# Attention scores computed by each head on its own half of the array's rows, with keys stored without zeros

## The chip, the cores and the metric

The kernel runs on one core of a Trainium2 chip. A core has a matrix engine (TensorE, in the profile PE, with its weight loads as PEld), a vector engine (DVE), a scalar engine (ACT), a general engine (POOL) and SyncE (SP), which here issues the transfers. Every engine works through its own instructions in order; semaphores tie them together. TensorE multiplies a stationary operand (up to 128 x 128, loaded first) by a moving operand (up to 512 columns) and leaves the sum in PSUM, a memory of eight banks per partition. A bank holds 512 float32 values in each of the 128 partitions. DVE and ACT read PSUM and write SBUF, from which TensorE reads.

The metric is device time in microseconds (us). The kernel before has a median of 1146.4 us in three runs (1146.05 to 1146.9).

## The reference

A trunk of four layers over x of 256 tokens by 1024 features, all float32. Each layer is a token mixer, then a squared-ReLU MLP of width 4096, both with an RMSNorm ahead and a residual sum behind. The mixers are, in order: differential attention (layers 0 and 3), MoBA attention (layer 1; with 256 tokens there is one block, so it is plain causal attention over 16 heads) and sliding-window attention with sinks (layer 2: 16 query heads, 2 key heads). All heads have 64 features. What the change touches is the product of queries and keys:

```python
HEAD_DIM = 64
# differential attention: 8 heads, each with two score maps
s = jnp.einsum('bqhcd,bkhcd->bhcqk', qi, k).astype(f32)
s = jnp.where(causal, s, -jnp.inf)
p = jax.nn.softmax(s, axis=-1)
p = p[:, :, 0] - lam * p[:, :, 1]
return jnp.einsum('bhqk,bkhe->bqhe', p.astype(v.dtype), v)
...
# MoBA: the own block
s_own = jnp.einsum('bhqd,bhkd->bhqk', qi, k_own).astype(f32)
...
# sliding window with sinks
s = jnp.einsum('bnqkgd,bnjkd->bnkgqj', qb, k2).astype(f32)
s = jnp.where(mask[None, :, None, None], s, -jnp.inf)
m = jnp.maximum(jnp.max(s, axis=-1, keepdims=True), sink)
e = jnp.exp(s - m)
p = (e / (jnp.sum(e, axis=-1, keepdims=True) + jnp.exp(sink - m))).astype(v.dtype)
```

So every layer has 16 score maps of 256 queries by 256 keys over 64 features.

## The kernel before

**Precision.** Every large product is made of three: an operand is split into a high part in the type float32r and the remainder, also float32r, and high x high, high x low and low x high are summed in PSUM. `stage` splits a weight piece of 1 MB in two halves of 128 x 1024 (ACT writes `whi`, line 80; DVE writes `wlo`, line 81). `put_q` and `put_k` do the same for queries and keys.

**A mixer layer.** `mixer_layer` runs projections with `proj` (line 296; 48 matmuls, two row blocks t of 24). Layers 0, 1 and 3 have six projections, four of which make the queries and keys of four heads c (`qk`, 512 columns), and two the values. Layer 2 has one for keys and values and four (256 columns) for queries. Behind each, DVE applies the rotary embedding (`rope`, lines 304 to 309). `turn` transposes the result on TensorE (`p_qk`, line 465), so that features lie on the partitions: partitions 0 to 63 hold one score map's features, 64 to 127 the other's. "Pair" is used here for the two maps that share a 128-partition tile; a pair is one `SC` step.

**Scores of a pair.** `new_keys` allocates two tiles `kpad` (high and low) and POOL fills with zeros the half of the partitions that is not a map's own (line 369). `put_k` copies each map's 64 partitions into its own block of columns. So a full 128-row matmul of a pair's queries with `kpad` gives both maps side by side: the zeros cancel the other map's features. Queries 0 to 127 see 128 keys, thus 256 columns; queries 128 to 255 see 256 keys, thus 512 columns. With three products each (`mm3`, lines 271 to 273) a pair costs six matmuls, into two banks `p_s0` and `p_s1`, one for each block of queries. For both maps and both query blocks, DVE adds the mask and reduces (`ns`, line 336), ACT takes the exponential with its sum (line 339). `diff_head` combines the two maps of a pair (lines 384 to 389), `head_block` divides by the sums (lines 424 to 427); `transposed` turns the result on TensorE (`p_t`, line 354), and the product with the values follows (`p_av`, lines 360 to 362 and 436). Line 436 writes one map's 64 output features to each half of the PSUM partitions: its matmuls use half of the array's columns each.

**Order.** The program text gives steps of attention out among the matmuls of the next projection: `proj` takes a list `midway`, run after its 24th matmul, and `plan` names for each projection what runs midway and what behind it: `QK` (transposes and splits), `SC` (scores and softmax), `TR` (transposes), `AV` (values), `OUT`. Layer 2 does it with `step`, `first` and `second`. A scheduler of the framework then settles each engine's order from this; the order of the built program differs from the text in places. The projections and the MLP share four banks `acc`; `p_qk`, `p_s`, `p_t`, `p_av`, `p_o` and `p_up` share four banks `wk`.

Of the kernel before, what the change touches and what calls it, by code (L numbers as in the profile page):

```python
# [12 lines left out]
F32R = mybir.dt.float32r  # L13
I32 = mybir.dt.int32
AF = mybir.ActivationFunctionType
OP = mybir.AluOpType
AX = mybir.AxisListType

P = 128
D = 1024  # L20
S = 256
NT = S // P
DEPTH = 4
FF = 4096
HD = 64
# [9 lines left out]
def f(ap):  # L35
    return ap.bitcast(F32)
# [3 lines left out]
def trunk(ctx: ExitStack, tc: tile.TileContext, xT, gains, lams, swa_row, fng, weights, out):  # L40
# [8 lines left out]
    def bank(tag, name):  # L49
        return ps.tile([P, 512], F32, tag=tag, name=name, bufs=4)  # L50

    def room(j, shape, name, dt=F32):

        return sb.tile(shape, dt, tag=f"slot{j}", name=name, bufs=1)
# [214 lines left out]
    def mm3(out, lh, ll, rh, rl, start, stop, **kw):  # L269

        T.matmul(out, lh, rh, start=start, stop=False, **kw)  # L271
        T.matmul(out, lh, rl, start=False, stop=False, **kw)  # L272
        T.matmul(out, ll, rh, start=False, stop=stop, **kw)  # L273
# [39 lines left out]
    def scores(q, k, mask, sinks):  # L313


        p0, p1 = bank("wk", "p_s0"), bank("wk", "p_s1")
        (qh, ql), (kh, kl) = q, k
        for p, t, n in ((p0, 0, P), (p1, 1, S)):
            o = p[:, :2 * n].rearrange("p (h m) -> p h m", h=2)
            a = slice(P * t, P * t + P)  # L320
            mm3(o, qh[:, a], ql[:, a], kh[:, :, :n], kl[:, :, :n], True, True)
        out = []
        if sinks is not None:
            es = tiny.tile([P, 2 * NT], F32, tag="es", name="es", bufs=2)
        scored[0] += 1
        pair_e = room(4 + scored[0] % 2, [P, 2, 3 * P], "e")
        ls = tiny.tile([P, 2 * NT], F32, tag="l", name="l", bufs=5)
        for c in range(2):
            ns = sb.tile([P, 3 * P], F32, tag="ns", name="ns", bufs=2)
            nm = tiny.tile([P, NT], F32, tag="nm", name="nm", bufs=4)  # L330
            l = ls[:, NT * c:NT * c + NT]
            e = pair_e[:, c]
            mk = mask[:, :, :].rearrange("p a b -> p (a b)")
            for t, p, n in ((0, p0, P), (1, p1, S)):
                s = slice(0, P) if t == 0 else slice(P, 3 * P)
                V.tensor_tensor_reduce(ns[:, s], p[:, n * c:n * c + n], mk[:, s], op0=OP.add, op1=OP.min,  # L336
                                       scale=-1.0, scalar=3.0e38 if sinks is None else sinks[c][1],
                                       accum_out=nm[:, t:t + 1])
                A.activation(e[:, s], ns[:, s], AF.Exp, bias=nm[:, t:t + 1], scale=-1.0,  # L339
                             accum_out=l[:, t:t + 1])  # L340
            if sinks is not None:
                A.activation(es[:, NT * c:NT * c + NT], nm, AF.Exp, bias=sinks[c][0])
            out.append((e, l))
        if sinks is not None:
            V.tensor_tensor(ls, ls, es, op=OP.add)
        return out, pair_e, ls
# [11 lines left out]
    def times_v(o, et, v):  # L358
# [1 line left out]
        T.matmul(o(0), et[:, 0:P], v(0), start=True, stop=True)  # L360
        T.matmul(o(1), et[:, P:2 * P], v(0), start=True, stop=False)
        T.matmul(o(1), et[:, 2 * P:3 * P], v(1), start=False, stop=True)

    def new_keys():

        kpad = [room(10 + x, [P, 2, 2, S], f"kpad{'hl'[x]}", F32R) for x in range(2)]
        for x in range(2):
            for h in range(2):
                G.memset(f(kpad[x][HD * (1 - h):HD * (1 - h) + HD, :, h, :]), 0.0)
        return kpad  # L370

    def part(b, n=1):

# [66 lines left out]
        V.tensor_tensor(both[:, 1], p[:, :S], f(both[:, 0]), op=OP.subtract)  # L440
        parts.append(both)

    line = []

    def step(block=None):


        line.append(block)
        if block is not None:
            next(block)  # L450
        if len(line) > 1 and line[-2] is not None:
            next(line[-2])
        if len(line) % 2 == 0:
            for x in line[:-2]:
                if x is not None:
                    next(x, None)
            line[:-2] = [None] * len(line[:-2])

    def turn(src, n):

        p = bank("wk", "p_qk")
        for b in range(n):
            for t in range(NT):
                at = S * b + P * t
                T.transpose(p[:, at:at + P], src(b, t), ident)  # L465
        return p[:, :S * n].rearrange("p (b m) -> p b m", m=S)
# [8 lines left out]
        V.scalar_tensor_tensor(q[1], p, 0.125, f(q[0]), op0=OP.mult, op1=OP.subtract)  # L475
        return q

    def put_k(k, p, n):
        for h in range(2):
            s = slice(HD * h, HD * h + HD)  # L480
            A.activation(k[0][s, :n, h, :], p[s], AF.Copy)
            V.tensor_tensor(k[1][s, :n, h, :], p[s], f(k[0][s, :n, h, :]), op=OP.subtract)

    def mixer_layer(i, n):
        mixer, slot = i % 3, i // 3
        r = norm_factor(n)
        parts = []
        kpad = new_keys()
        if mixer == 2:
            bias = room(8, [P, 1024], "bias")  # L490
            rest = room(9, [P, 1024], "rest")
# [7 lines left out]
                V.scalar_tensor_tensor(kv[:, t, :], p[t], r[:, t:t + 1], rest[:, :256],  # L499
                                       op0=OP.mult, op1=OP.add)  # L500
            rope(kv[:, :, 0:P].rearrange("p t (s e) -> p t s e", e=HD), 2)
            put_k(kpad, turn(lambda b, t: kv[:, t, 0:P], 1), 1)
            kT = [x[:, 0] for x in kpad]
            first, second = [], []
            for c in range(4):
                p = proj(n, (256, 1), False, first)
                qn = room(c % 2, [P, NT, 256], "qn")
                for t in range(NT):
                    for h in range(2):
                        s = slice(P * h, P * h + P)  # L510
                        o = qn[:, t, :].rearrange("p (b h e) -> p b h e", h=2, e=HD)[:, :, h, :]
                        bs = bias[:, 512 * h + P * c:512 * h + P * c + P]
                        V.scalar_tensor_tensor(o, p[t][:, s].rearrange("p (b e) -> p b e", e=HD), r[:, t:t + 1],
                                               bs.rearrange("p (b e) -> p b e", e=HD), op0=OP.mult, op1=OP.add)
                rope(qn[:, :, :].rearrange("p t (s e) -> p t s e", e=HD), 4)
                for do in second:
                    do()
                qs = []

                def block(b, c=c, qs=qs, qn=qn):  # L520
                    if b == 0:
                        qs += put_q(turn(lambda b, t: qn[:, t, P * b:P * b + P], 2))
                    h = 2 * c + b
                    step(head_block(
                        parts, [x[:, b] for x in qs], kT, lambda m: kv[:, m, P:2 * P], band,
                        [(sink[:, h + 8 * s:h + 8 * s + 1], nsink[:, h + 8 * s:h + 8 * s + 1]) for s in range(2)],
                        h,
                    ))

                first, second = [lambda f=block: f(0)], [lambda f=block: f(1)]  # L530
        else:
            v = [room(8 + j, [P, NT, 512], f"v{j}") for j in range(2)]
            vdone = 0
            qk, qs, heads, pairs, ets, els = {}, {}, {}, {}, {}, {}

            def QK(c):

                qs[c] = put_q(turn(lambda j, t: qk[c][:, t, P * j:P * j + P], 2))
                put_k(kpad, turn(lambda j, t: qk[c][:, t, P * (2 + j):P * (2 + j) + P], 2), 2)

            def vh(h):
                return lambda m: v[h // 4][:, m, P * (h % 4):P * (h % 4) + P]

            def SC(h):
                q, k = [x[:, h % 2] for x in qs[h // 2]], [x[:, h % 2] for x in kpad]
                if mixer == 0:
                    if h % 2 == 0:
                        els[h // 2] = tiny.tile([P, 2 * NT], F32, tag="el", name="el")
                    heads[h] = diff_head(slot, q, k, els[h // 2][:, NT * (h % 2):NT * (h % 2) + NT])
                else:  # L550
                    heads[h] = head_block(parts, q, k, vh(h), causal, None, h)
                next(heads[h])
# [15 lines left out]
            def LAM(_):  # L568
                if i == 0:
                    lambdas()  # L570

            order = (0, 1, "v", 2, 3, "v") if mixer else (0, 1, "v", 2, "v", 3)
            plan = [[], [], [(QK, 0), (LAM, 0), (SC, 0)], [(SC, 1)], [(TR, 0), (QK, 1), (SC, 2)], [(TR, 1), (SC, 3)],
                    [(TR, 2)], [(TR, 3), (AV, 0), (AV, 1)], [(QK, 2), (SC, 4)], [(AV, 2), (AV, 3), (SC, 5)],
                    [(TR, 4), (QK, 3), (SC, 6)], [(TR, 5), (SC, 7)],
                    [(AV, 4), (AV, 5), (TR, 6), (TR, 7), (AV, 6), (AV, 7)]]
            if mixer == 0:
                plan[6:8] = [[(TR, 2), (AV, 0)], [(TR, 3), (AV, 1)]]
                plan[8:] = [[(AV, 2), (QK, 2), (OUT, 0), (SC, 4)], [(AV, 3), (SC, 5)], [(TR, 4), (AV, 4)],
                            [(OUT, 1), (TR, 5), (AV, 5)],  # L580
                            [(QK, 3), (SC, 6), (SC, 7), (OUT, 2), (TR, 6), (AV, 6), (TR, 7), (AV, 7)]]
            for at, c in enumerate(order):
# [16 lines left out]
            return parts, (lambda: OUT(3))  # L599
        for do in first + second:  # L600
            do()
        for _ in range(3):
            step()
        line.clear()
        return parts, lambda: None


# [295 lines left out]
```

## Time and profile before

| | |
|---|---|
| median of three runs | 1146.4 us |
| the profiled execution, whole | 1146.28 us |
| its span, first to last instruction | 1144.3 us |
| TensorE clock granted | 0.998 |
| moved by DMA | 198.66 MB |

A row of instructions reads: source line, engine, operation, tile written <- tiles read, partitions x elements, count, then busy time and mean duration. In a timeline the first two numbers are start and duration in us. Durations on TensorE overlap: a matmul starts before the one ahead of it has drained, so the cost of one is the distance to the start of the next. On DVE and ACT too a row starts a little before the row ahead has ended.

### The profile page before, as it was taken

Reading aid. Unit: us, or ns where it says so; the run is one execution under the profiler, and the core shown is the slowest. Engines: PE = TensorE matmul, PEld = TensorE weight load, DVE = VectorE, ACT = ScalarE, POOL = GpSimd, SP = SyncE. Lnnn points to the kernel's source line nnn. Section 1 sums busy time; section 2 is a strip of 40 time slices with the busy share of each in tenths; the row PEclk is TensorE's granted clock in tenths of the full one; section 3 lists DMA queues with packets and bytes.
Section 4 is the critical chain, followed back from the end, with each engine's and each line's share of the span. In section 5 each row is a group of like instructions: output and inputs, shape, how many; then the busy total and the mean of one; then the engine's idle time right before and its main releaser. Section 6 shows DMA issues by size and latency. Waiting matters only on the chain.

```text
span 1144.3 us, 17044 instructions
## 1 busy us (share of the span) xinstructions
PE 1133.7 (99%) x6560; PEld 987.0 (86%) x6560; DVE 827.9 (72%) x1608; ACT 660.6 (58%) x1207; POOL 11.4 (1%) x39
## 2 busy tenths in 40 slices
PE   9999999999999999999999999999999999999997
PEld 7789888888888888888899898888888889888886
DVE  7978977656676698766569887775667788777454
ACT  6866655544476665654446765554447676665342
POOL 1000000000000000000000000000000000000000
PEclk9999999999999999999999999999999999999999
DMA  9543455555544355555553346555553435555551
GB/s 327 198 147 117 165 201 190 194 201 185 185 141 148 117 184 187 195 200 191 184 208 111 111 148 221 184 185 189 188 202 127 151 139 164 192 195 169 186 182 37
DMA packets 30608, 198.66 MB, mean 174 GB/s; under 512 B 3520, under 2 KB 5184, under 8 KB 7360
## 3 DMA queue, kind: packets, MB, share of 16 engines
q1 hardware_dynamic: 30240, 197.06, 50.0%
q8 instruction: 51, 0.84, 0.3%
q10 hardware_dynamic: 288, 0.52, 0.1%
q14 instruction: 29, 0.24, 0.1%
HBM read 196.52 MB, written 1.05 MB: 173 GB/s over the span
## 4 chain that ended last, share of the span: by engine, by line
PE 95%; DVE 2%; DMA 1%; ACT 1%; issue 0%; SPq 0%; DVEq 0%
PE p_up L610 21%; PE p_in L296 18%; PE p_down L610 15%; PE p_up L611 11%; PE p_down L611 8%; PE p_last L273 3%; PE p_last L271 3%; PE p_last L272 3%; PE p_d L273 2%; PE p_d L272 2%; PE p_d L271 2%; PE p_t L354 1%; PE p_s L271 1%; PE p_qk L465 1%; DVE wlo L81 1%; PE p_av L436 1%
## 5 line engine op out<-in xcount | busy, mean ns | idle before, releaser
L81 DVE TENSOR_TENSOR wlo<-raw,whi 128x1024 fp32r<-128x1024 f32 (+1 forms) x374 | 447.0, 1209 | 206.0 <-ACT whi L80 204.9
L80 ACT ACTIVATE whi<-raw 128x1024 fp32r<-128x1024 f32 (+1 forms) x374 | 384.5, 1046 | 213.3 <-issue 111.1
L610 PE MATMUL p_up<-hg,whi 128*128 128x512 f32 x1024 | 356.9, 393 | 0.4
L611 PE MATMUL p_up<-hg,wlo 128*128 128x256 f32 x1024 | 284.9, 279 | 0.0
L610 PE MATMUL p_down<-uu,whi 128*128 128x512 f32 x768 | 266.4, 392 | 0.0
L610 PEld LDWEIGHTS p_up<-hg,whi 128*128 128x128 f32 x1024 | 191.5, 187 | 43.3 <-DVE hg L229 1.0
L611 PE MATMUL p_down<-uu,wlo 128*128 128x256 f32 x768 | 214.3, 279 | 0.0
L296 PE MATMUL p_in<-whi,hg 128*128 128x512 f32 (+1 forms) x736 | 211.3, 371 | 0.0
L611 PEld LDWEIGHTS p_up<-hg,wlo 128*128 128x128 f32 x1024 | 193.2, 189 | 0.5
L610 PEld LDWEIGHTS p_down<-uu,whi 128*128 128x128 f32 x768 | 143.7, 187 | 32.1
L296 PEld LDWEIGHTS p_in<-whi,hg 128*128 128x128 f32 x736 | 132.3, 188 | 22.8 <-DVE hg L229 0.6
L611 PEld LDWEIGHTS p_down<-uu,wlo 128*128 128x128 f32 x768 | 144.8, 189 | 0.0
L296 PE MATMUL p_in<-wlo,hg 128*128 128x512 f32 (+1 forms) x368 | 130.4, 369 | 0.5 <-DVE wlo L81 0.5
L685 ACT ACTIVATE uu<-u 128x512 fp32r<-128x512 f32 x64 | 40.5, 633 | 71.1 <-DVE u L683 71.1
L296 PEld LDWEIGHTS p_in<-wlo,hg 128*128 128x128 f32 x368 | 68.8, 189 | 12.7 <-DVE wlo L81 1.7
L616 ACT ACTIVATE cross<-p_up 128x256 f32<-128x256 f32 x128 | 47.9, 374 | 39.3 <-PE p_up L611 33.8
L228 ACT ACTIVATE hg<-hT,gn 128x256 fp32r<-128x256 f32 x64 | 31.6, 503 | 65.5 <-DVE hT L629 65.2
L339 ACT ACTIVATE e<-ns,nm 128x128 f32<-128x128 f32 (+1 forms) x128 | 56.9, 446 | 12.0 <-DVE nm L336 11.7
L686 DVE TENSOR_TENSOR uu<-u,uu 128x512 fp32r<-128x512 f32 x64 | 44.2, 691 | 21.5 <-ACT uu L685 21.5
L271 PE MATMUL p_d<-oo,whi 128*128 128x256 f32 x192 | 55.1, 287 | 0.0
L272 PE MATMUL p_d<-oo,whi 128*128 128x256 f32 x192 | 55.1, 287 | 0.0
L617 DVE TENSOR_TENSOR relu<-p_up,cross 128x256 f32<-128x256 f32 x128 | 53.5, 418 | 1.6 <-ACT cross L616 1.5
(182 smaller groups left out, 1246.3 us busy)
## 6 DMA issues: line engine op xcount, KB each, us to landing
raw<-in_weights SPq DMA_DIRECT2D x181, 1024.0 KB, 4.9
raw<-in_weights SPq DMA_DIRECT2D x8, 256.0 KB, 4.5
raw<-in_weights SPq DMA_DIRECT2D x4, 512.0 KB, 7.7
hT<-in_xT SPq DMA_DIRECT2D x8, 128.0 KB, 4.4
bias<-in_swa_row SPq DMA_DIRECT2D x1, 512.0 KB, 4.3
grow<-in_fng SPq DMA_DIRECT2D x1, 512.0 KB, 3.5
out<-res SPq DMA_DIRECT2D x4, 128.0 KB, 2.1
out<-res ACTq DMA_DIRECT2D x2, 256.0 KB, 2.2
```

Of the source, the lines that this page charges most:

```text
L80: A.activation(hi[:, s], raw[:, s], AF.Copy)
L81: V.tensor_tensor(lo[:, s], raw[:, s], f(hi[:, s]), op=OP.subtract)
L271: T.matmul(out, lh, rh, start=start, stop=False, **kw)
L272: T.matmul(out, lh, rl, start=False, stop=False, **kw)
L273: T.matmul(out, ll, rh, start=False, stop=stop, **kw)
L296: T.matmul(out[t], n.both[k // 2][:, k % 2, x, P * t:P * t + P], r3(kb)(parts[k // kb][w])[:, k % kb, :], start=fresh, stop=k == 7 and x + ...
L339: A.activation(e[:, s], ns[:, s], AF.Exp, bias=nm[:, t:t + 1], scale=-1.0, accum_out=l[:, t:t + 1])
L610: T.matmul(r3(2)(p), hi, x, start=start, stop=False, skip_group_check=True)
L611: T.matmul(p[:, :S], lo, x[:, 0], start=False, stop=stop, skip_group_check=True)
L616: A.activation(cross, p[:, S:], AF.Copy)
L617: V.tensor_tensor(out, p[:, :S], cross, op=OP.add)
L686: V.tensor_tensor(both[:, :, 1], r3(2)(u), f(both[:, :, 0]), op=OP.subtract)
```

## The change

Each map's scores are computed with its own 64 partitions of queries and keys alone, on half of the array's rows; the two maps of a pair write different banks, `ps_h[0]` and `ps_h[1]`, and stand alternately in the text. Keys are stored as they come from the transposes, without zeros, in one tile `khl`, and two buffers of it alternate. In the order, the two pairs of a head group are given out together (`SC` of both midway); layer 2 loses `step` and gives transposes and scores of two pairs out in `blocks_of`, the values in `values_of`.

```diff
     def scores(q, k, mask, sinks):
-        p0, p1 = bank("wk", "p_s0"), bank("wk", "p_s1")
+        ps_h = [bank("wk", f"p_s{c}") for c in range(2)]
         (qh, ql), (kh, kl) = q, k
-        for p, t, n in ((p0, 0, P), (p1, 1, S)):
-            o = p[:, :2 * n].rearrange("p (h m) -> p h m", h=2)
+        for cols, t, n in ((slice(0, P), 0, P), (slice(P, 3 * P), 1, S)):
             a = slice(P * t, P * t + P)
-            mm3(o, qh[:, a], ql[:, a], kh[:, :, :n], kl[:, :, :n], True, True)
+            for x, y, first, last in ((qh, kh, True, False), (qh, kl, False, False), (ql, kh, False, True)):
+                for c in range(2):
+                    r = slice(HD * c, HD * c + HD)
+                    T.matmul(ps_h[c][:, cols], x[r, a], y[r, :n], start=first, stop=last, skip_group_check=True)
...
-            for t, p, n in ((0, p0, P), (1, p1, S)):
+            for t in range(NT):
                 s = slice(0, P) if t == 0 else slice(P, 3 * P)
-                V.tensor_tensor_reduce(ns[:, s], p[:, n * c:n * c + n], mk[:, s], op0=OP.add, op1=OP.min,
+                V.tensor_tensor_reduce(ns[:, s], ps_h[c][:, s], mk[:, s], op0=OP.add, op1=OP.min,
...
-    def new_keys():
-
-        kpad = [room(10 + x, [P, 2, 2, S], f"kpad{'hl'[x]}", F32R) for x in range(2)]
-        for x in range(2):
-            for h in range(2):
-                G.memset(f(kpad[x][HD * (1 - h):HD * (1 - h) + HD, :, h, :]), 0.0)
-        return kpad
...
-    def put_k(k, p, n):
-        for h in range(2):
-            s = slice(HD * h, HD * h + HD)
-            A.activation(k[0][s, :n, h, :], p[s], AF.Copy)
-            V.tensor_tensor(k[1][s, :n, h, :], p[s], f(k[0][s, :n, h, :]), op=OP.subtract)
+    kput = [0]
+
+    def put_k(p, n):
+        kput[0] += 1
+        both = room(10 + kput[0] % 2, [P, 2, n, S], "khl", F32R)
+        k = [both[:, 0], both[:, 1]]
+        A.activation(k[0], p, AF.Copy)
+        V.tensor_tensor(k[1], p, f(k[0]), op=OP.subtract)
+        return k
...
-                qs = []
-
-                def block(b, c=c, qs=qs, qn=qn):
-                    if b == 0:
-                        qs += put_q(turn(lambda b, t: qn[:, t, P * b:P * b + P], 2))
-                    h = 2 * c + b
-                    step(head_block(
...
-                first, second = [lambda f=block: f(0)], [lambda f=block: f(1)]
+                def blocks_of(c=c, qn=qn):
+                    qs = put_q(turn(lambda b, t: qn[:, t, P * b:P * b + P], 2))
+                    for x in heads[-2:]:
+                        next(x)
+                    for b in range(2):
+                        h = 2 * c + b
+                        heads.append(head_block(
...
+                        next(heads[-1])
+
+                def values_of(c=c):
+                    for x in heads[2 * c - 2:2 * c] if c else []:
+                        next(x, None)
+
+                first, second = [blocks_of], [values_of]
...
-            plan = [[], [], [(QK, 0), (LAM, 0), (SC, 0)], [(SC, 1)], [(TR, 0), (QK, 1), (SC, 2)], [(TR, 1), (SC, 3)],
-                    [(TR, 2)], [(TR, 3), (AV, 0), (AV, 1)], [(QK, 2), (SC, 4)], [(AV, 2), (AV, 3), (SC, 5)],
-                    [(TR, 4), (QK, 3), (SC, 6)], [(TR, 5), (SC, 7)],
-                    [(AV, 4), (AV, 5), (TR, 6), (TR, 7), (AV, 6), (AV, 7)]]
+            plan = [[], [], [(QK, 0), (LAM, 0), (SC, 0), (SC, 1)], [],
+                    [(QK, 1), (TR, 0), (TR, 1), (SC, 2), (SC, 3)], [], [(TR, 2)], [(TR, 3), (AV, 0), (AV, 1)],
+                    [(QK, 2), (SC, 4), (SC, 5)], [(AV, 2), (AV, 3)], [(QK, 3), (TR, 4), (TR, 5), (SC, 6), (SC, 7)],
+                    [], [(AV, 4), (AV, 5), (TR, 6), (TR, 7), (AV, 6), (AV, 7)]]
             if mixer == 0:
-                plan[6:8] = [[(TR, 2), (AV, 0)], [(TR, 3), (AV, 1)]]
-                plan[8:] = [[(AV, 2), (QK, 2), (OUT, 0), (SC, 4)], [(AV, 3), (SC, 5)], [(TR, 4), (AV, 4)],
+                plan[6:] = [[(TR, 2), (AV, 0)], [(TR, 3), (AV, 1)],
+                            [(AV, 2), (QK, 2), (OUT, 0), (SC, 4), (SC, 5)], [(AV, 3)], [(TR, 4), (AV, 4)],
                             [(OUT, 1), (TR, 5), (AV, 5)],
                             [(QK, 3), (SC, 6), (SC, 7), (OUT, 2), (TR, 6), (AV, 6), (TR, 7), (AV, 7)]]
```

More of the change, by code (lines that the diff above doesn't have):

```diff
@@ L441, in head_block @@
         parts.append(both)
[L443 to L457, printed above, removed]
     def turn(src, n):
@@ L487, in mixer_layer @@
         parts = []
-        kpad = new_keys()
         if mixer == 2:
@@ L501, in mixer_layer @@
             rope(kv[:, :, 0:P].rearrange("p t (s e) -> p t s e", e=HD), 2)
-            put_k(kpad, turn(lambda b, t: kv[:, t, 0:P], 1), 1)
-            kT = [x[:, 0] for x in kpad]
-            first, second = [], []
+            kT = [x[:, 0] for x in put_k(turn(lambda b, t: kv[:, t, 0:P], 1), 1)]
+            heads, first, second = [], [], []
             for c in range(4):
@@ L517, in mixer_layer @@
                     do()
-                qs = []
-                def block(b, c=c, qs=qs, qn=qn):
-                    if b == 0:
-                        qs += put_q(turn(lambda b, t: qn[:, t, P * b:P * b + P], 2))
-                    h = 2 * c + b
-                    step(head_block(
[L525 to L528, printed above, removed]
-                first, second = [lambda f=block: f(0)], [lambda f=block: f(1)]
+                def blocks_of(c=c, qn=qn):
[5 more added lines that the diff above has]
+                        heads.append(head_block(
+                            parts, [x[:, b] for x in qs], kT, lambda m: kv[:, m, P:2 * P], band,
+                            [(sink[:, h + 8 * s:h + 8 * s + 1], nsink[:, h + 8 * s:h + 8 * s + 1]) for s in range(2)],
+                            h,
+                        ))
+                        next(heads[-1])
[3 more added lines that the diff above has]
+                first, second = [blocks_of], [values_of]
         else:
@@ L533, in mixer_layer @@
             vdone = 0
-            qk, qs, heads, pairs, ets, els = {}, {}, {}, {}, {}, {}
+            qk, qs, ks, heads, pairs, ets, els = {}, {}, {}, {}, {}, {}, {}
             def QK(c):
                 qs[c] = put_q(turn(lambda j, t: qk[c][:, t, P * j:P * j + P], 2))
-                put_k(kpad, turn(lambda j, t: qk[c][:, t, P * (2 + j):P * (2 + j) + P], 2), 2)
+                ks[c] = put_k(turn(lambda j, t: qk[c][:, t, P * (2 + j):P * (2 + j) + P], 2), 2)
             def vh(h):
@@ L544, in SC @@
             def SC(h):
-                q, k = [x[:, h % 2] for x in qs[h // 2]], [x[:, h % 2] for x in kpad]
+                q, k = ([x[:, h % 2] for x in y[h // 2]] for y in (qs, ks))
                 if mixer == 0:
@@ L601, in mixer_layer @@
             do()
-        for _ in range(3):
-            step()
-        line.clear()
+        for x in heads[-2:] * 2:
+            next(x, None)
         return parts, lambda: None
```

## The prediction

> **What bounds the kernel now.** I read the page first: busy time by engine, the slices and the chain of work that ended last.
>
> ```profile
> span 1144.3 us, 17044 instructions
> PE 1133.7 (99%) x6560; PEld 987.0 (86%) x6560; DVE 827.9 (72%) x1608; ACT 660.6 (58%) x1207; POOL 11.4 (1%) x39
> ...
> PE 95%; DVE 2%; DMA 1%; ACT 1%; issue 0%; SPq 0%; DVEq 0%
> ```
>
> TensorE sets the end: 99% busy, 95% of the chain. So an edit counts by the TensorE time that it takes or frees, and by the waits that it puts before TensorE's next instruction. Waits are rare now. The list of who waited for whom has one for scores, 0.6 us in layer 0; the other engines have slack as a mean over the span. The table by stretches (length, then busy time of PE, PEld, DVE, ACT, POOL) says where they have little, in layer 2:
>
> ```profile
> 616.00:626.00 10.00, 10.00 (x80) 9.56 (x79) 9.22 (x32) 7.50 (x23) 0.00 (x0) 1.00 0.30 105
> 626.00:636.00 10.00, 9.98 (x83) 8.98 (x82) 9.37 (x36) 8.21 (x27) 0.00 (x0) 1.00 0.33 107
> ...
> PE p_s L271 <- issue: 0.6, 1, 0.6
> ```
>
> DVE is busy 9.2 and 9.4 of 10 us there. TensorE does not wait because the present order spreads the scores over the projection. That is the place to watch.
>
> **The change part by part.** *Scores as they are.* A pair that runs without a break, then the next instructions:
>
> ```profile
> 622.38 0.28 PE L271 MATMUL p_s<-kpadh,qhl 128*128 128x256 f32 x1
> 622.50 0.28 PE L272 MATMUL p_s<-kpadl,qhl 128*128 128x256 f32 x1
> 622.62 0.28 PE L273 MATMUL p_s<-kpadh,qhl 128*128 128x256 f32 x1
> 622.74 0.40 PE L271 MATMUL p_s<-kpadh,qhl 128*128 128x512 f32 x1
> 622.98 0.40 PE L272 MATMUL p_s<-kpadl,qhl 128*128 128x512 f32 x1
> 623.21 0.39 PE L273 MATMUL p_s<-kpadh,qhl 128*128 128x512 f32 x1
> 623.44 0.28 PE L296 MATMUL p_in<-whi,hg 128*128 128x256 f32 x1
> 623.56 0.28 PE L296 MATMUL p_in<-wlo,hg 128*128 128x256 f32 x1
> ```
>
> From start to start 256 columns cost 0.12, 512 cost 0.23; a pair costs 623.44 - 622.38 = 1.06 us. Four layers have 32 pairs: 33.9 us removed.
>
> *Scores as they will be.* Twelve matmuls per pair, six of 128 columns and six of 256, on alternating row halves. No row here uses halves of the rows. The nearest are the value products of layers 1 and 2, on halves of the columns, and their neighbours:
>
> ```profile
> 132.97 0.59 PE L264 MATMUL p_row<-acc,ones 128*128 128x256 f32 x2
> ...
> L264 PE MATMUL p_row<-acc,ones x6: 378/378/379, 133.0 to 679.0; 128*128 128x256 f32 x6
> ...
> 352.64 0.71 PE L354 MATMUL p_t<-ident,e 128*128 128x128 f32 x5
> 353.28 1.52 PE L436 MATMUL p_av<-et,v 128*64 128x256 f32 x16
> 354.73 0.50 PE L296 MATMUL p_in<-whi,hg 128*128 128x512 f32 x1
> 355.06 0.40 PE L296 MATMUL p_in<-wlo,hg 128*128 128x512 f32 x1
> 355.30 0.39 PE L296 MATMUL p_in<-whi,hg 128*128 128x512 f32 x1
> ...
> 60.77 0.39 PE L360 MATMUL p_av<-v,et 128*128 128x128 f32 x2
> 60.99 0.39 PE L361 MATMUL p_av<-v,et 128*128 128x128 f32 x2
> ```
>
> One full-array float32 instruction of 256 columns takes about 0.21 (two in 0.59, of which 0.38 is the second's own duration), one of 128 takes 0.11 (two from 60.77 to 60.99). The sixteen at 353.28 are eight of each: 8 x 0.21 + 8 x 0.11 = 2.6 us one after the other; they took 1.52. So halves of the columns run two at a time, weight loads included. I take the same for row halves: two matmuls in one slot, as long as the slot of a 128-column weight load, 0.11 to 0.12 whether the moving side has 128 or 256 columns (60.77 and 622.38 above); I use 0.113. 192 slots are 21.7 us. Bounds: if the loads of the two halves follow each other, 43.4; if a 128-column float32r matmul cost 0.22, like the two float32 instructions at 60.77 together, 96 slots grow by 0.11, +10.6.
>
> The Trainium skill says the same in TensorEngine Tiling (Array Packing), Key Properties: different tiles load weights and multiply in parallel. The row above agrees for columns; no run here shows it for rows.
>
> *Entering and leaving.* A 128-column matmul lasts 0.27 (the row at 102.35 below), so the last of the transposes starts at 352.64 + 0.71 - 0.27 = 353.08; the next could start at 353.19; `p_av` starts at 353.28: 0.09 late. Behind `p_av` the same: last start 354.53, expected 354.64, found 354.73; and the instruction after that comes 0.33 later instead of 0.23, because its load was not done ahead. All eight excursions to column halves look so. A row half loads 128 columns, not 64, so I count 0.2 in and 0.2 out, 0.4 per excursion (bounds 0 and 0.4). In the built program the 384 score matmuls stand in 28 runs: seven of 24, six groups in two runs, three in three, because the scheduler puts projections where it takes operands or banks to be late. 28 x 0.4 = 11.2 us; runs that start with one half alone, or have three of one half in a row, lose 1.5 us more. Sum on TensorE: 21.7 + 1.5 + 11.2 = 34.4 against 33.9: +0.5 us. The halving is eaten by the excursions.
>
> *Keys.* Per call one ACT and one DVE copy fewer, and no memsets. These ended no TensorE wait but the one above, and POOL has 1% to do: nothing gained on the path, except that keys are ready some 1.2 us sooner, which is counted below. Two buffers of keys free `QK` from waiting for scores. No transfer is moved.
>
> *Both pairs at once.* Here I expect the loss. Four `wk` banks of scores come to DVE together; the transposes, which stand next in TensorE's order, wait for DVE. One place worked out, layer 2, second query projection. What each piece costs DVE, from start to next start (where the next row is not shown, the duration less the 0.08 by which rows overlap):
>
> ```profile
> 616.38 1.22 DVE L81 TENSOR_TENSOR wlo<-raw,whi 128x1024 fp32r<-128x1024 f32 x1
> 617.52 0.16 DVE L345 TENSOR_TENSOR l<-l,es 128x4 f32<-128x4 f32 x1
> 617.59 1.22 DVE L81 TENSOR_TENSOR wlo<-raw,whi 128x1024 fp32r<-128x1024 f32 x1
> ...
> 620.75 0.35 DVE L336 CUSTOM_DVE_ANT_0 ns<-p_s,band,rest 128x128 f32<-128x128 f32 x1
> ...
> 622.10 1.12 DVE L513 SCALAR_TENSOR_TENSOR qn<-p_in,nr,bias 128x128 f32<-128x128 f32 x4
> 623.14 0.34 DVE L336 CUSTOM_DVE_ANT_0 ns<-p_s,band,rest 128x128 f32<-128x128 f32 x1
> ...
> 624.12 0.28 DVE L304 TENSOR_TENSOR ropea<-qn,cc 128x128 f32<-128x128 f32 x1
> 624.32 0.17 DVE L424 RECIPROCAL rl<-l 128x4 f32<-128x4 f32 x1
> 624.41 0.14 DVE L425 RECIPROCAL rl<-l 128x2 f32<-128x2 f32 x1
> 624.46 0.20 DVE L305 TENSOR_TENSOR ropeb<-qn,nsn 128x64 f32<-128x64 f32 x1
> 624.58 0.95 DVE L427 TENSOR_TENSOR e<-e,rl 128x768 f32<-128x768 f32 x1
> 625.45 0.22 DVE L307 TENSOR_TENSOR ropeb<-qn,sn 128x64 f32<-128x64 f32 x1
> ...
> 625.99 0.28 DVE L309 TENSOR_TENSOR qn<-ropea,ropeb 128x128 f32<-128x128 f32 x1
> ```
>
> In the built order DVE has, between the low part of the queries (which the scores need) and the end of the rotary embedding (which the next `p_qk` needs): four `qn` 1.04, one `wlo` 1.14, eight reductions 2 x 1.35 = 2.70 (620.75 to 622.10 are four), the rotary's first three 0.20 + 0.12 + 0.14, the sums 0.08 + 0.09 + 0.05, the division 0.87, the rotary's last 0.20: 6.63 us. TensorE has from the same moment ten slots 1.13, leaving 0.2, 32 projections at 0.12: 5.17. So `p_qk` waits about 1.5 us, and behind it stand six transposes and 16 projection matmuls that need nothing. In the built order of the present kernel 37 projections and six transposes stand between.
>
> A second place, the tail of layers 0 and 3, from the last score to the first transpose of its result:
>
> ```profile
> 99.42 0.39 PE L273 MATMUL p_s<-kpadh,qhl 128*128 128x512 f32 x1
> ...
> 100.12 0.60 PE L412 MATMUL p_o<-ident,o 128*128 128x128 f32 x4
> ...
> 102.35 0.27 PE L354 MATMUL p_t<-ident,e 128*128 128x128 f32 x1
> ```
>
> 19 `p_d` and these four cover 2.9 us; the built order keeps 12 and four, 0.8 us less cover over the same eight reductions and exponentials, in two layers: 0.6 to 0.8 each. With every engine's built order laid side by side and the durations of such rows, I find further waits of 0.2 to 0.8 us at some fifteen places: scores waiting for a bank, `p_av` and `p_t` for copies and softmax. Less the waits that are there now, layer 2 loses 4 us, layers 0 and 3 2.3 each, layer 1 1.2: an estimate of +10. Bounds: -1 (cover as good as now and the one wait for keys gone) and +24 (1.5 in each of 16 groups).
>
> Sum on the profiled execution, 1144.3 and the 2.0 us around the span, 1146.3: + 0.5 + 10 = 1156.8. It stands 0.1 below the median of the runs, so from the median I say 1157.
>
> **The rivals.** (a) *The halving shows.* Excursions cost nothing, because a load for rows can be fetched ahead, and the waits stay as now: 21.7 + 1.5 - 33.9 = -10.7, 1135.7 us. For it: full-array loads are fetched ahead everywhere. Against: eight excursions of eight cost, and the built order has the shorter cover. It takes both at once: with excursions free but the waits there, TensorE comes sooner to the same late operands, waits longer, and the loss only falls to about +7. The Trainium skill's TensorEngine Tiling (Array Packing), Theoretical Speedup, allows up to twice the speed for a contraction of 64; that would be half of 33.9, 17 us.
>
> (b) *A draw.* Excursions 0.4, waits no longer than now: +0.5, 1147 us. For it: TensorE hardly waits in the present order, made by the same scheduler. Against: the two places above.
>
> (c) *Row halves load one after the other.* 384 x 0.113 + 11.2 = 54.6, +20.7; TensorE then reaches the transposes later and the new waits shrink to a few tenths: 1167.5. For it: no row shows halves of the rows. Against: halves of the columns.
>
> (d) *128 columns cost 0.22.* +10.6 on top of +0.5, the waits shrinking to about 6: 1163.5. For it: no float32r matmul here is narrower than 256. Against: the load alone explains 0.11 at both widths.
>
> **How the numbers follow.** The forecast has 0.66, its own range 1150 to 1162 (the wait estimate from 3 to 15); (a) 0.08, (b) 0.08, (c) 0.12, (d) 0.06. The range 1150 to 1169 takes in (c) and (d) and leaves out (a), (b) and some edges, 0.18. What a measurement can tell from no change is about 0.2%, 2.3 us. Faster by more is (a) with the best edge of the forecast, 0.09; within it (b), 0.08; slower 0.83.
>
> **What would show it.** Score rows of the two halves starting within some ns of each other, a slot of 0.11: right; 0.22 from slot to slot: (c) or, for 128 columns alone, (d). The first instruction behind a run of scores about 0.09 late and its successor another 0.1: excursions right; none: (a). Waits of `p_qk` for line 309's successor in layer 2 of 1 to 2 us, and of `p_t` for DVE in the tails of layers 0 and 3: the burst is right. If layer 2 from first projection to first `p_up` is no longer than now, the wait estimate was wrong, and if the four mixer stages together are shorter, so is the forecast.

## The result, and the profile after

| | median, us | runs | ratio to before (95%) |
|---|---|---|---|
| before | 1146.22 | 4 | |
| after | 1159.87 (1157.49 to 1160.8) | 4 | 1.0113 (1.0101 to 1.0125) |

The change costs 13.6 us; 1157 was forecast. These lines of the page after stand against those of before:

```profile
span 1159.0 us, 17346 instructions
PE 1140.6 (98%) x6752; PEld 989.4 (85%) x6752; DVE 821.1 (71%) x1595; ACT 654.6 (56%) x1194; POOL 3.1 (0%) x23
...
PE 90%; DVE 4%; ACT 3%; DMA 1%; issue 1%; SPq 0%; DVEq 0%; ACTq 0%
```

TensorE has fallen from 95% to 90% of the chain, DVE and ACT have risen from 3% to 7% together: TensorE now waits for them. The list of who waited for whom (total us, times, longest) names the places:

```profile
PE p_qk L444 <- DVE qn L309: 2.1, 2, 1.3
PE p_s L324 <- DVE o L402: 2.0, 2, 1.0
...
PE p_av L431 <- DVE nm L339: 0.8, 2, 0.6
PE p_t L357 <- ACT e L342: 0.7, 1, 0.7
PE p_qk L444 <- DVE qk L309: 0.7, 1, 0.7
PE p_av L431 <- ACT v L576: 0.6, 1, 0.6
...
PE p_t L357 <- ACT et L358: 0.5, 1, 0.5
```

The rows above alone are 7.4 us; all entries but the warm-up's 1.0 come to 9.0. Before, they came to 1.7, with two entries for `p_qk` and `p_s` of 0.6 each and one of 0.5 for `wlo`, which both kernels have:

```profile
PE p_qk L465 <- DVE qk L309: 0.6, 1, 0.6
```

The matmul rows around a group of 24 in layer 2, without a break, show what the scores themselves cost:

```profile
635.90 0.84 PE L357 MATMUL p_t<-ident,e 128*128 128x128 f32 x6 [0.50 <-ACT et L358]
636.67 1.66 PE L324 MATMUL p_s<-khl,qhl 64*128 64x128 f32 x24
638.26 0.39 PE L296 MATMUL p_in<-whi,hg 128*128 128x256 f32 x1
638.48 0.28 PE L296 MATMUL p_in<-wlo,hg 128*128 128x256 f32 x1
638.60 0.40 PE L296 MATMUL p_in<-whi,hg 128*128 128x256 f32 x2
```

Twenty-four matmuls occupy 638.26 - 636.67 = 1.59 us, twelve slots of 0.13 with the exit: the two halves do run two at a time. Full rows would need 2 x 1.06. The instruction behind has its successor 0.22 later instead of 0.12: the load that was not done ahead.

The longest single wait is that of `p_qk` in layer 2, 1.3 us. The next stands in the last score group of layer 0:

```profile
98.21 1.12 PE L324 MATMUL p_s<-khl,qhl 64*128 64x128 f32 x13
100.33 0.92 PE L324 MATMUL p_s<-khl,qhl 64*128 64x128 f32 x9 [0.99 <-DVE o L402]
...
103.53 0.33 PE L357 MATMUL p_t<-ident,e 128*128 128x128 f32 x1 [0.28 <-DVE e L383]
```

The second pair waits 0.99 us for a bank of `wk`, which the value product holds until line 402 has read it. By the program text half rows need both banks of a pair in the first slot, where full rows needed the second bank three matmuls later. The same wait stands in layer 3, and there the granted clock (the column behind the busy times) falls:

```profile
945.00:950.00 5.00, 4.24 (x22) 4.05 (x23) 4.47 (x26) 4.15 (x17) 0.00 (x0) 0.57 0.16 67
950.00:955.00 5.00, 5.00 (x35) 4.90 (x34) 1.38 (x3) 1.74 (x4) 0.00 (x0) 0.75 0.00 0
```

Clock 0.57 and 0.75 over 5 us each are 5 x 0.43 + 5 x 0.25 = 3.4 us of clock lost. About 2.4 us of it reached the time: from the wait's end to the first value products of line 364 the same matmuls took 953.53 - 945.76 = 7.77 us here and 105.67 - 100.33 = 5.34 us in layer 0, where the clock was full and one transpose waited. The four runs fit: 1160.8, 1159.92 and 1159.81 us at a mean clock of 0.995 to 0.996, 1157.49 us at 0.998.

### The profile page after: what moved, and what is told of

The parts are those of the page before. It is cut to its first block, busy times and chain, and to the rows that moved or that the text cites. A ratio compares the mean times of both kernels' runs of the same rounds, so it can differ in the third digit from the quotient of the medians.

```text
span 1159.0 us, 17346 instructions
## 1 busy us (share of the span) xinstructions
PE 1140.6 (98%) x6752; PEld 989.4 (85%) x6752; DVE 821.1 (71%) x1595; ACT 654.6 (56%) x1194; POOL 3.1 (0%) x23
## 4 chain that ended last, share of the span: by engine, by line
PE 90%; DVE 4%; ACT 3%; DMA 1%; issue 1%; SPq 0%; DVEq 0%; ACTq 0%
PE p_up L597 20%; PE p_in L296 16%; PE p_down L597 15%; PE p_up L598 10%; PE p_down L598 8%; PE p_last L273 3%; PE p_last L271 3%; PE p_last L272 3%; PE p_s L324 2%; DVE wlo L81 1%; PE p_d L273 1%; PE p_d L272 1%; PE p_d L271 1%; PE p_t L357 1%; DMA raw<-in_weights 1%; ACT e L342 1%
## 5 line engine op out<-in xcount | busy, mean ns | idle before, releaser
L271 PE MATMUL p_d<-oo,whi 128*128 128x256 f32 x192 | 56.4, 294 | 0.0
L272 PE MATMUL p_d<-oo,whi 128*128 128x256 f32 x192 | 56.2, 293 | 0.0
L273 PE MATMUL p_d<-oo,wlo 128*128 128x256 f32 x192 | 54.8, 288 | 0.0
```

## The experiments

Three theories stood at the start. *Theory 1*, that of the prediction: half rows about break even, since each excursion costs 0.4 us, and the loss is in waits that come from giving two pairs out together. *Theory 2*: the half rows are the loss. *Theory 3*: the clock is. "Planner" is the scheduler that settles each engine's order; a "stretch" is an unbroken row of score matmuls in the built program, each one excursion (the expectations below call it a run). Theory 3 can be the smaller part only: the one run at 0.998 still stands 11.3 us above before.

**Half rows in the old order.** `scores`, `put_k` and `khl` of the change, with `plan` and `step` of the kernel before.

```diff
-            plan = [[], [], [(QK, 0), (LAM, 0), (SC, 0), (SC, 1)], [],
+            plan = [[], [], [(QK, 0), (LAM, 0), (SC, 0)], [(SC, 1)], [(TR, 0), (QK, 1), (SC, 2)], [(TR, 1), (SC, 3)],
...
+                    step(head_block(
```

> Half rows and keys without zeros alone: the steps are given out as in the kernel before (one pair at a time). Theory 1 (the loss of the change is mainly in waits from giving two pairs out together; half rows pay 0.4 us per entry into and exit from halves of the rows): the built program has 46 runs of score matmuls instead of 28, so 21.7 + 1.5 + 46 x 0.4 = 41.6 against 33.9 us, +7.7: 1154 us, and no wait of p_qk for DVE in layer 2. Theory 2 (the half rows themselves are the loss, the order is free): the cost per run would then be (11.3 + 12.2 - 1.5) / 28 = 0.79 us instead of 0.4, and 46 runs give 1146.2 - 10.7 + 36.1 = 1172 us. Theory 3 (most of the loss is the drop of the clock): 1147 to 1150 us with a clock of 0.998.

Measured 1162.1 us (1161.08 to 1164.93), 15.9 above before. Theory 1 misses it by 8, theory 2 by 10, theory 3 by 12 or more. All four runs had a mean clock below 0.998 (0.992 to 0.997), so some of the 15.9 us is the clock: 3.4 us were lost in the profiled run, as the last section shows.

**The order alone.** The new `plan` and `blocks_of`, with `scores`, `new_keys` and `put_k` of before.

```diff
-        ps_h = [bank("wk", f"p_s{c}") for c in range(2)]
+        p0, p1 = bank("wk", "p_s0"), bank("wk", "p_s1")
...
+            mm3(o, qh[:, a], ql[:, a], kh[:, :, :n], kl[:, :, :n], True, True)
```

> The order of the change alone: both pairs of a group given out together, but scores of the kernel before (full rows, keys with zeros). Theory 1: the excursions are gone and the waits stay, +10 us: 1156 us, between 1152 and 1160, with waits of p_qk for line 309's DVE in layer 2 of about 1 to 1.5 us. Theory 2: 1146 to 1148 us. Theory 3: 1146 to 1148 us, unless the clock drops here too (then 3.4 us more).

Measured 1147.57 us, ratio 1.0011 (1.0002 to 1.002): +1.4, not +10. Its waits on the chip, whole but for the warm-up's 1.0:

```profile
PE p_qk L449 <- DVE qk L309: 0.7, 1, 0.7
PE p_s L271 <- issue: 0.6, 1, 0.6
PE p_in L296 <- DVE wlo L81: 0.5, 1, 0.5
PE p_up L600 <- DVE hg L229: 0.2, 1, 0.2
```

No `p_qk` waits for `qn`. Theory 1's reason has fallen: two pairs given out together do not make the waits. Yet the waits are in the kernel after, so they come with the half rows, in either order.

**Fewer excursions, twice.** In the changed kernel, and in the run with the old order, the product with the low part of the keys moves to the front. It is ready last, so a stretch then no longer breaks off behind its first matmuls.

```diff
-            for x, y, first, last in ((qh, kh, True, False), (qh, kl, False, False), (ql, kh, False, True)):
+            for x, y, first, last in ((qh, kl, True, False), (ql, kh, False, False), (qh, kh, False, True)):
```

> The changed kernel with one thing moved: of the three products of a pair the one with the low part of the keys stands first instead of second, and the high times high last. The built program then has 19 runs of score matmuls instead of 28. Theory 1: 9 x 0.4 = 3.6 us of excursions less. If nothing takes it back 1156 us; if the waits behind the runs take back what TensorE gains (the operands come no sooner) 1158 to 1160 us. Theory 2 (0.79 per run): 7 us less, 1153 us. Theory 3: 1160 us, or 1156.5 where the clock does not drop.

> As the first of these runs (half rows, one pair at a time in the order of the kernel before), with the product with the low part of the keys first: 32 runs of score matmuls, one for each pair, instead of 46. Theory 1: 21.7 + 1.5 + 32 x 0.4 = 36.0 against 33.9 us: +2.1, 1148 us, and 5.6 us below the first run. Theory 2 (0.79 per run): 1146.2 - 10.7 + 25.3 = 1161 us, 11 us below the first run. Theory 3: as the first run.

Measured 1153.72 us (1153.07 to 1157.11) and 1157.15 us (1156.59 to 1158.06). In the old order 14 stretches fewer gave 4.95 us, 0.35 for each. That is net of two things that moved beside it: in the profiled runs all waits but the warm-up's come to 10.3 us where they were 8.3, and the clock lost 1.7 us (0.66 from 100 to 105 us) instead of 3.4. With both taken out of the 5.8 us between the spans it is about 0.4. Theory 2's 0.79 is out (it wanted 11 us), 0.4 is about right. In the new order 9 stretches gave 6.15 us, of which some 2.4 can be the clock, full in this profile. But both kernels still stand 9 to 11 us above what excursions explain.

**Wider, and so cheaper?** Where those 9 us come from, the trace of the run with the low part first shows in layer 2. Its matmuls from the first scores to the next `p_qk`, 31 projections behind the scores (first and last shown):

```profile
611.85 0.44 PE L324 MATMUL p_s<-khl,qhl 64*128 64x128 f32 x3
612.21 0.38 PE L296 MATMUL p_in<-whi,hg 128*128 128x256 f32 x1
612.58 1.53 PE L324 MATMUL p_s<-khl,qhl 64*128 64x128 f32 x21
614.04 0.39 PE L296 MATMUL p_in<-wlo,hg 128*128 128x256 f32 x1
...
617.74 0.28 PE L296 MATMUL p_in<-wlo,hg 128*128 128x256 f32 x1
619.32 0.66 PE L444 MATMUL p_qk<-ident,qn 128*128 128x128 f32 x4 [1.31 <-DVE qn L309]
```

TensorE's list runs out at 617.74 and it waits 1.31 us for the rotary embedding. With full rows and the same program text 37 projections stood there, and the scores took longer. Theory 4: the planner reckons the 128-column matmuls as long ones, and so takes little work to be needed behind them. To test it, TensorE must get the same work in a form that the planner reckons otherwise. Queries 0 to 127 take all 256 keys; the additional 128 columns are computed and not read.

```diff
-        for cols, t, n in ((slice(0, P), 0, P), (slice(P, 3 * P), 1, S)):
+        for cols, t, n in ((slice(0, S), 0, S), (slice(S, 2 * S), 1, S)):
...
-                V.tensor_tensor_reduce(ns[:, s], ps_h[c][:, s], mk[:, s], op0=OP.add, op1=OP.min,
+                V.tensor_tensor_reduce(ns[:, s], ps_h[c][:, S * t:S * t + P * (t + 1)], mk[:, s], op0=OP.add, op1=OP.min,
```

> The run with the keys' low part first (1153.7 us), with one thing added: queries 0 to 127 are multiplied with all 256 keys, not 128 (the further 128 columns are not read). The order alone cost 1.4 us and half rows alone 15.9, so the waits do not come from giving two pairs out together. Theory 4, new: they come from the planner, which settles every engine's order by its own durations and seems to hold the 128-column matmuls for long ones: it puts the weight split wlo ahead of the reductions and leaves fewer projections behind the scores. With 256 columns its built order has the split behind the reductions. TensorE's slot stays at 0.11 (the load decides it), so 16 groups of 24 at 0.09 in, 1.48, 0.09 out and 0.11 behind are 28.3 us, 4 further runs 1.2: 29.5 against 33.9; with 2 to 4 us of waits left 1144 to 1147 us. Rival, theory 5: the waits are the latency from scores over DVE and ACT to the transposes, which shows because half rows are done sooner; widening changes nothing: 1152 to 1155 us, more if 256 columns cost a longer slot (96 slots).

> The changed kernel with 256 columns for queries 0 to 127 as its one edit; the built program has 36 runs of score matmuls instead of 28. Theory 4: 28.3 us for 16 groups and 20 further runs at 0.3, 34.3 against 33.9; with 2 to 4 us of waits 1148 to 1151 us, in spite of 8 more excursions. Theory 5: 8 more excursions at 0.36, thus 1160 to 1163 us.

> Half rows, one pair at a time in the order of the kernel before, keys' low part first (1157.2 us so far), with 256 columns for queries 0 to 127; 34 runs of score matmuls instead of 32. A pair in a run of its own costs 0.09 + 0.79 + 0.09 + 0.11 = 1.08 us, as much as full rows (1.06). Theory 4: 1147 to 1151 us. Theory 5: 1157 to 1159 us.

| | 128 columns | 256 columns |
|---|---|---|
| changed kernel | 1159.87 | 1152.83 (1152.55 to 1153.3) |
| low part first | 1153.72 | 1144.87 (1144.53 to 1145.34) |
| old order, low part first | 1157.15 | 1150.60 (1150.32 to 1150.98) |

Twice the columns, and 6.6 to 8.9 us less in all three, although each has more stretches than its neighbour (36 for 28, 20 for 19, 34 for 32). Some of the left column is the clock, which was full in all runs of the right one: the changed kernel's run at 0.998 leaves 4.7 us, that of the old order (1156.59 us) 6.0. Theory 5 has fallen. The same place in layer 2, with 256 columns:

```profile
608.72 0.50 PE L324 MATMUL p_s<-khl,qhl 64*128 64x256 f32 x3
609.15 0.38 PE L296 MATMUL p_in<-whi,hg 128*128 128x256 f32 x1
...
609.82 1.58 PE L324 MATMUL p_s<-khl,qhl 64*128 64x256 f32 x21
611.33 0.39 PE L296 MATMUL p_in<-wlo,hg 128*128 128x256 f32 x1
...
615.86 0.40 PE L296 MATMUL p_in<-whi,hg 128*128 128x256 f32 x2
616.28 0.63 PE L444 MATMUL p_qk<-ident,qn 128*128 128x128 f32 x4
```

The 21 scores take 611.33 - 609.82 = 1.51 us instead of 1.46, so wider is hardly dearer on the chip. From the first score to `p_qk` it is 7.56 us here and 619.32 - 611.85 = 7.47 there: DVE's work is as long as ever. What differs is TensorE's list: 39 projections behind the scores and 4 between them, instead of 31 and one; the list has no wait for `p_qk` here. The lists of waits show it for the whole kernel. With the low part first and 128 columns:

```profile
PE p_s L324 <- DVE o L402: 3.0, 2, 1.5
PE p_qk L444 <- DVE qn L309: 1.9, 2, 1.3
PE p_qk L444 <- DVE qk L309: 1.3, 2, 0.7
...
```

and with 256 (warm-up left out):

```profile
PE p_s L324 <- DVE o L402: 0.9, 2, 0.5
PE p_qk L444 <- DVE qk L309: 0.7, 1, 0.7
PE p_in L296 <- DVE wlo L81: 0.5, 1, 0.5
PE p_up L597 <- DVE hg L229: 0.2, 1, 0.2
PE p_t L357 <- ACT e L342: 0.2, 1, 0.2
```

With 128 columns the rows of `p_s`, `p_qk`, `p_t` and `p_av` came to 9.6 us (3.0, 3.2, 2.0 and 1.4), here to 1.8: 7.8 us of the 8.9. The expectation named a second sign, the weight split `wlo` behind the reductions. That was wrong: it stands ahead of them in both traces. It does stand behind them with full rows, in the run with the order alone:

```profile
618.86 0.28 DVE L309 TENSOR_TENSOR qn<-ropea,ropeb 128x128 f32<-128x128 f32 x1
619.07 1.22 DVE L81 TENSOR_TENSOR wlo<-raw,whi 128x1024 fp32r<-128x1024 f32 x1
```

There DVE takes 618.86 - 613.04 = 5.8 us from the queries' low part to the rotary's last instruction; with half rows 7.2 us (from 611.83 to 618.98, and from 608.70 to 615.85 with 256 columns), of which the split is 1.13. So against full rows the half rows of 128 columns lost on both engines, more work of DVE under fewer projections; the 256 columns gave back the projections alone, and that was enough.

The changed kernel with 256 columns came out 2 us above its range; 16 more stretches than with the low part first cost 7.96 us there, 0.50 each, above the 0.4 that the prediction reckoned with.

**Is it the weight split all the same?** The run with the low part first, 128 columns, and DVE's reductions and ACT's exponentials preferred by the planner.

The lines below the added one are only indented:

```diff
+        with tc.high_priority(300):
             for c in range(2):
...
                     V.tensor_tensor_reduce(ns[:, s], ps_h[c][:, s], mk[:, s], op0=OP.add, op1=OP.min,
```

> The run with the keys' low part first and 128 columns (1153.7 us), in which the planner is told to prefer the reductions and exponentials of the scores to other work of DVE and ACT. Theory 4 in its narrow form (the harm is the weight split put ahead of reductions that could start): most of the 8.8 us that 256 columns gave, 1145 to 1148 us. Theory 4 in its wide form (the planner holds the scores for unfinished, so no precedence helps, and TensorE's own order has too little behind them): 1151 to 1154 us. Theory 5: no change.

Measured 1154.11 us (1152.93 to 1155.71): nothing gained in the time. The clock hides some of it: all five runs had 0.995 to 0.997, against 0.998 or 0.999 in four of the five before the edit, and the waits came to 8.9 us instead of 10.9. Even so the gain is 2 to 3 us by estimate from these figures, not most of 8.8. The split still starts ahead of the reductions in layer 2 (615.05, the first reduction at 616.18), and `p_qk` still waits 1.28 us there. That fits the wide form; why the preference did not move the split, no run shows.

**Two steps further.** Layer 2 went back to full rows and keys with zeros; then, in layers 0 and 3, the transposes and values of heads 4 and 5 were given out together, so that the last group is not broken. The second edit:

```diff
-                            [(AV, 2), (QK, 2), (OUT, 0), (SC, 4), (SC, 5)], [(AV, 3)], [(TR, 4), (AV, 4)],
-                            [(OUT, 1), (TR, 5), (AV, 5)],
+                            [(AV, 2), (QK, 2), (OUT, 0), (SC, 4), (SC, 5)], [(AV, 3)], [(TR, 4), (TR, 5), (AV, 4), (AV, 5)],
+                            [(OUT, 1)],
```

> The run with keys' low part first and 256 columns (1144.9 us), with layer 2 back to full rows and keys with zeros, both pairs still given out together. Layer 2 took 75.2 us there, 73.8 with the order alone and full rows, 74.4 before. If half rows lose in layer 2 (each group has a p_t or p_av, itself in another mode or waiting, as neighbour): 0.8 to 1.4 us less, 1143.5 to 1144.1 us. If the loss there was the planner's order for that layer: no change, 1144.5 to 1145.3 us.

> As the run before, and in layers 0 and 3 the transposes and values of heads 4 and 5 are given out together, behind the values projection's first half; the last group of scores then stands whole: 12 runs of 24, instead of 14 runs. Two excursions at 0.3 to 0.4 us less, and the 0.6 us wait of the last six scores for a bank is gone or moves: 0 to 1.5 us less, 1142.5 to 1144 us. If the wait for the bank (freed by line 402's DVE) grows as in the kernel with the low part first (1.5 us in each tail): 1 to 2 us more, 1145 to 1146 us.

Measured 1143.47 us, ratio 0.9971 (0.996 to 0.9981), and 1143.18 us, ratio 0.997 (0.9958 to 0.9981), against 1146.61 us for the kernel before beside them. The first gained 1.4 us over 1144.87, as layer 2's lengths had said; the second's further 0.3 us is within the spread. Its wait for the bank is gone, and other waits took its place:

```profile
PE p_qk L458 <- DVE qk L309: 1.7, 3, 0.7
PE p_t L364 <- DVE e L397: 1.1, 2, 0.6
```

So half rows do pay where three conditions meet: whole groups of 24, the late product first, and an order that leaves TensorE work behind them. With any one of them missing the table has 1150.60, 1152.83 and 1153.72 us, all above before. In layer 2 they did not pay even so. An unbroken group of the run with 256 columns took 378.63 - 377.01 = 1.62 us with its exit (layer 1); with 0.09 in and 0.11 behind it is 1.82, and twelve groups save 12 x (2 x 1.06 - 1.82) = 3.6 us. From 1147.6 for the order alone to 1143.2 it is 4.4.

## Why the prediction came close, and where its reason was wrong

The median lies 2.9 us above the forecast, within the range. In part that was luck. The span grew by 14.7 us: the waits by 7.3 (9.0 for 1.7) where +10 was forecast, the clock took 2.4 to 3.4 that nobody forecast, and some 4 to 5 us are left for TensorE's own work, where the forecast had +0.5. An excess in one term and a shortage in two others came near to cancelling. From the first projection to the first `p_up` the four mixers grew by 3.6, 1.3, 4.8 and 5.0 us, the last with the clock in it. The steps one by one:

*What bounds it, and layer 2 as the tight place*: right. The mixer of layer 2 went from 74.4 to 79.2 us, where +4 of waits was forecast.

*Two halves at a time, slot 0.113*: right; rivals (c) and (d) are out. 128 float32r columns carry no penalty in these traces: widening them made the 21 scores 0.05 longer, not shorter.

*Excursions at 0.4*: right in kind, and near in size: 0.35 and 0.50 in the two pairs of runs that vary little else, where 0.4 was held to be the upper bound. At 0.50 the 28 stretches cost 2.8 us more than the sum had, and the order alone has another 1.4; that is most of what TensorE's own term lacked. The Trainium skill's TensorEngine Tiling (Array Packing), Key Properties, says that a change of the tiling mode drains the engine; the trace agrees, with 0.22 instead of 0.12 behind the exit at 638.26. The page gives no price.

*Keys cost nothing*: not tried alone, so it stays open. The step from the order alone to half rows with 256 columns, keys included, is -2.7 us, where slots and excursions alone were reckoned at 29.5 - 33.9 = -4.4.

*"Both pairs at once. Here I expect the loss."* This is the step that failed. Given out together with full rows, the pairs cost 1.4 us. The size of the waits was near, because it was read off the built order: the 1.5 us forecast for the second query projection were measured as 1.3 by the list of waits. But a built order has causes, and I took the text of `plan` for the cause, when the same text with full rows does not make the waits and a wider form of the half rows takes most of them away. I had the clue in the prediction: 32 projections where 37 stood before, a shorter cover although TensorE would be sooner. Had I asked why, the forecast could have said that the loss is not inherent.

*Tails of layers 0 and 3*: 0.6 to 0.8 us were forecast at the first transpose. Found were 0.28 there, and 0.99 ahead of it for a bank; the wait for a bank in this place was not in the sum.

*The clock*: not foreseen. 3.4 us lost, of which 2.4 reached the time.

One chain of runs adds up the whole change, each step a median: 1146.2 before; order alone +1.4; half rows of 256 columns in whole groups -2.7; 128 instead of 256 columns +8.9; the late product second instead of first +6.1, of which some 2.4 is the clock; 1159.9. The steps hold in this sequence; the smaller ones would differ in another.

Shown is that the number of columns alone, at an equal slot on the chip, moves the built order and 6.6 to 8.9 us, 4.7 to 8.9 where the clock is taken out. That the planner's own durations are the reason is inferred from the order: those durations stand in no profile.

## What to carry to other kernels

Where a scheduler settles the order, a change of an instruction's shape can also change the order that it builds, and by more than the instruction's own time. If waits appear behind it, count the work that stands behind it before and after, and try the same work in another shape. Halves of the array paid here only in long unbroken stretches: one excursion costs 0.35 to 0.5 us here, the gain of one pair, so order the operands by when they are ready and put the latest first. And take the parts of a change one at a time: this one hides a gain of 2.7 us behind a loss of 15.

## What the runs showed of the hardware that was not expected

The granted clock halved for about 7 us after a wait of TensorE of about 1 us among other short ones: in the tail of layer 3 in the kernel after, in that of layer 0 in the run with half rows in the old order (first column the window, the clock third from the right):

```profile
95.00:100.00 5.00, 3.98 (x33) 3.25 (x31) 4.65 (x22) 1.40 (x7) 0.00 (x0) 0.90 0.61 216
100.00:105.00 5.00, 5.00 (x26) 4.78 (x24) 4.33 (x21) 3.54 (x15) 0.00 (x0) 0.50 0.00 0
105.00:110.00 5.00, 5.00 (x40) 4.90 (x39) 1.20 (x1) 3.27 (x7) 0.00 (x0) 0.92 0.03 7
```

That costs 5 x (0.10 + 0.50 + 0.08) = 3.4 us again. At half the clock a loss of 3.4 us means 6.8 us of time; in the old order with the low part first it was half of that (1.7 us lost). It does not follow each time: layer 0 of the kernel after has the same 0.99 us wait at full clock, and the profiled run of the new order with the low part first waits 1.5 us in both tails at full clock, with TensorE busy for only 3.40 and 3.29 of the 5 us. The Trainium skill's TensorE: Matmul & The Clock Gate, Part 1, ties the drop to an idle window of some 3.4 us that runs freely, whenever the kernel started; here the drop came with waits far shorter, at a TensorE busy share of 3.98 of 5 us. What decides it stays open.
